# One hybrid decoder step: norm in five steps, old x loaded in two parts, the scan's filling work in token halves, state products over 128 rows

## The chip, the cores and the metric

The kernel runs on one core of one Trainium2 chip. The metric is the device time of one execution in microseconds, as the median over runs. A core has five engines that work through instruction lists of their own: TensorE (PE, matmuls; its weight loads are listed as PEld), VectorE (DVE), ScalarE (ACT), GpSimd (POOL) and SyncE (SP), which here only issues DMAs.

## The reference

One step of a decoder of two layers, for a prompt of 512 tokens and 8 sequences of 8 sample tokens, so T = 576 tokens in all, in fp32. Each layer is FFN, token mixer, FFN; the mixer of layer 0 is a Mamba-2 scan (SSD), that of layer 1 is windowed attention. Each of the six sublayers stands between two norms:

```python
hin = modulated_norm(x, norm_pre[i, s], mod[:, :, s])      # rms_norm, then scale and shift
f = swiglu(hin, w_in, w_out)                               # or ssd_mixer, or swa_mixer
x = x + FFN_RES * mod[:, :, s, 2] * rms_norm(f, norm_post[i, s])
```

In the scan, the prompt goes in 4 chunks of 128 tokens, and the 8 sample sequences start from states of their own. Per group of heads (4 groups) the state after a chunk is

```python
chunk_states = einsum('bclgn,bclgrp->bcgrpn', Bc, xc * decay_to_end[..., None])
hc = hc * a + s
```

and the outputs are y, the new states, the last conv inputs and the new key and value buffers.

## The kernel before

**Data and products.** Activations lie feature-major: 128 partitions by 8 feature blocks by tokens. The tokens are cut in two halves, HALF = ((0, 256), (256, 320)); the 64 sample tokens are the last ones of half 1. Each fp32 operand is split into a high and a low part, and a product is three matmuls (low weight by high activation, high by low, high by high); so a gemm of 8 blocks is 24 matmuls of one half's columns (line 501, output tile `g` in one of 4 PSUM buffers), and one of 6 blocks is 18. `load_w` brings a weight block from memory (tile `raw`, two buffers, issued on SP), ACT casts the high part (line 469) and DVE subtracts to get the low part (line 472); where the weights of several items are held at once, the tiles are called `wx` (otherwise `whi`, `wlo`).

**Who orders.** The Tile scheduler sets a fixed order for each engine at build time, by its own costs and by the order in which the code asks for things; at run time each engine goes through its list in that order and waits where an operand or a buffer is not there yet.

**A sublayer.** An FFN is four groups of feature tiles. The first goes through `run_in`: the weights of 8 items are held, all 8 are run over half 0, then all over half 1, and each gemm is followed by its `use`: for a gate, a Silu on ACT (line 724); for an up projection, a product on DVE (`sil`, 729), a cast on ACT (730) and a difference on DVE (`mid`, 731). The other groups go through `seven` (block products with fewer multiplications, line 673). The last group ends in `run_out` with r = 8: 8 blocks of w_out are held and run over half 0, then half 1; each result is added into `f` (566) and its sums of squares are begun (`stat`: lines 327 to 349, on ACT, POOL and DVE).

**The boundary.** Class `Boundary` leads from one sublayer to the next. `open` allocates tiles and loads the old x (1 MB for half 0, 1 MB for the first part of half 1, 256 KB for its samples, on SP, line 94); `stat`, `sums` form the norm's sums without waiting for the last product (gram matmuls of f and old x, line 343); `update(h)` adds f to x and writes the next sublayer's `hin` on DVE and ACT (lines 407 to 449). `update(0)` runs inside `run_out`, while PE works on half 1. `update(1)` runs inside the next `run_in`, ahead of its items in code: first the samples' part, then four pairs of feature blocks, each f times b1 (414), x plus f (415), two `pn` (436), two `hin` (438 on ACT, 439 on DVE):

```python
        if bd:
            bd.update(1)
            bd.close()
        for h in (0, 1):
```

PE meanwhile runs the items' half 0, which needs only half 0 of `hin`.

**The scan.** For each of 4 groups, a generator `mix` runs the scan's steps and yields nine times: after the B and C transposes, after each of 4 prompt chunks, after `old(0)`, `new(0)`, `old(1)` and `new(1)`. `old(q)` loads four sequences' states `h0` and multiplies C by them (`pos`, 994); `new(q)` makes their new states: for each sequence two matmuls over all sample tokens, the sequence picked by the mask in `bm`, into `psts` (1009 the high part, 1010 the low part over 64 rows), a scaling of h0 on POOL (1013) and a sum on DVE (1016). Between the yields the loop takes whole items from a list `fill`: projections of this and of the next group with their convolution (POOL copies at lines 846 to 867) and blocks of the output product. `gate_mul` and `gate_sum` (lines 1060 to 1075, sum of squares `gsq` by a matmul, 234) are called at two of these yields.

Of the kernel before, what the change touches and what calls it, by code (L numbers as in the profile page):

```python
# [10 lines left out]
F32 = mybir.dt.float32  # L11
# [30 lines left out]
PSP = 512  # L42
NX = 1
NG = 2
GK = 6
GJ = 2
GA = 0
GB = 1
GC = 1
# [9 lines left out]
def body(ctx: ExitStack, tc: tile.TileContext, A, O):  # L59
# [30 lines left out]

    def x_copy(d, x, store):
        for t, (o, n) in zip(x, XO):
            a, b = d[:, o:o + n], t.rearrange("p k n -> p (k n)")
            nc.sync.dma_start(a if store else b, b if store else a)
# [201 lines left out]
    class Boundary:  # L296
# [7 lines left out]

        def open(self):
            l, s = self.l, self.s
            state["xp_cm"] = tc.tile_pool(name=f"xpool{l}{s}", bufs=1, side="right", reuse_waits="tile")
            state["xp"] = state["xp_cm"].__enter__()
            x_cur[:] = x_alloc()
            x_copy(x_dram if l or s else A["xT"], x_cur, False)  # L310
            self.cms = [tc.tile_pool(name=f"{n}{l}{s}", bufs=1, side="right", reuse_waits="tile") for n in ("upd", "stats")]
            self.pool, pool = (cm.__enter__() for cm in self.cms)
            self.spool = pool
            mod_gate(l, s, self.mv)
            self.ns = 1 if self.end else 2
# [80 lines left out]

        def update(self, h):
            f, b1 = self.f, self.b1
            if not self.end:
# [3 lines left out]
            if self.end:  # L403
                return self.finish(h)
            if h == 1:
                ts = self.pool.tile([128, 8, 64], F32, tag="ts", name="ts", bufs=1)
                V.tensor_tensor(out=ts, in0=f[1][:, :, 256:320], in1=b1[:, 256:320].unsqueeze(1).to_broadcast([128, 8, 64]),
                                op=ALU.mult)
                V.tensor_tensor(out=x_cur[2], in0=x_cur[2], in1=ts, op=ALU.add)
                if not self.end:  # L410
                    norm_sample(self.pool, self.nmv, b2, self.hin)
            for kk in range(0, 8, 2):
                fs, xs = f[h][:, kk:kk + 2, 0:256], x_cur[h][:, kk:kk + 2, :]
                V.tensor_tensor(out=fs, in0=fs, in1=b1[:, 0:256].unsqueeze(1).to_broadcast([128, 2, 256]), op=ALU.mult)
                V.tensor_tensor(out=xs, in0=xs, in1=fs, op=ALU.add)
                if not self.end:
                    norm_prompt(self.pool, self.nmv, b2, self.hin, h, (kk, kk + 1))

        def finish(self, h):
# [97 lines left out]
    def run_in(hin, items, first, ex, pend, between=None, pre=()):  # L517
# [5 lines left out]
              for i, (src, _) in enumerate(items[:first])]  # L523
        if bd:
            bd.update(1)
            bd.close()
        for h in (0, 1):
            if between and h:
                between()
            for i, (w, (_, use)) in enumerate(zip(ws, items)):  # L530
                if h == 0 and i < len(pre):
                    use(h, gemm_part(w, hin_acts(hin, h), HALF[h][1], range(4, 8), pre[i][1]))
                else:
                    use(h, gemm(w, hin_acts(hin, h), HALF[h][1]))
            if bd and h == 0:
                bd.place(1, base)
        for src, use in items[first:]:
# [15 lines left out]
    def run_out(loads, acts, f, first, bd=None, r=0, ex=None, bias=None):  # L553
# [22 lines left out]
        if r:  # L576
            ws = [load_w(src, n, ex if i >= WR else None) for i, (src, n, _) in enumerate(loads[nl:])]
            todo = [(w, w0, o) for w, (_, _, os_) in zip(ws, loads[nl:]) for o, w0 in os_]
            for a in todo:
# [128 lines left out]
    def ffn(l, s, hin, f, pend, bd):  # L708
        si = 0 if s == 0 else 1
        sub = lambda name: tc.tile_pool(name=f"{name}{l}{s}", bufs=1, reuse_waits="tile")  # L710
        with sub("mid") as mp:
# [52 lines left out]
            with sub("tail") as tp:  # L764
                bd.open()
                run_out(loads, halves(mids), f, False, bd, RF, borrow(tp, "wf", 2 * (RF - WR), mk * 128))


    def ssd(l, hin, f, pend, bd):
        with ExitStack() as cx:  # L770
# [122 lines left out]
            def mix(g, d, y, sa, se, dtt, cd):  # L893
# [111 lines left out]
                def new(q, xh, xl):  # L1005

                    for b in range(q * 4, q * 4 + 4):
                        pst = ps_s.tile([128, 512], F32, tag="s", name="psts")
                        PE.matmul(out=pst, lhsT=bm[:, b, :], rhs=xh, start=True, stop=False)
                        PE.matmul(out=pst, lhsT=bm[0:64, b, :], rhs=xl, start=False, stop=True)  # L1010
                        h0 = h0s.pop(b)
# [4 lines left out]
                        V.tensor_tensor(out=h0, in0=pst, in1=h0, op=ALU.add)  # L1016
                        nc.scalar.dma_start(O["ssm_s"][g, :, b], h0)

                for i in range(5):
                    bcs(i)  # L1020
                yield
                h = None
                for i in range(4):
                    h = chunk(i, h)
                    yield
                skip(slice(0, NP))
                xd, pyv = within(4)
                old(0)
                yield
                xh = R2.tile([128, 512], F32R, tag="xdd", name="xh", bufs=2)  # L1030
                xl = R2.tile([64, 512], F32R, tag="xl", name="xl", bufs=1)
                S.copy(xh, xd)
                V.tensor_tensor(out=xl, in0=xd[0:64], in1=xh[0:64].bitcast(F32), op=ALU.subtract)
                new(0, xh, xl)
                yield
# [4 lines left out]
                yield  # L1040
                new(1, xh, xl)
                yield

# [58 lines left out]
            R = tc.tile_pool(name="ssdr", bufs=1, reuse_waits="tile")  # L1102
            Rcm, R = R, R.__enter__()
            def run1(item):
                run_in(hin, [item()], 0, None, pend)

# [12 lines left out]
            for g in range(4):  # L1119
                last = g == 3  # L1120
                fill = []
                outs = [lambda ld=ld, yn=yn: run_out([ld], yn_acts(yn), f, g == 1) for ld in out_loads(g - 1)] if g else []
                zt, ynew = [], []

                def z_run(j):
# [6 lines left out]
                    run1(lambda: z_item(g, j, zt[j]))  # L1132

                zs = [lambda j=j: z_run(j) for j in range(4)]
                dn, nxt = proj_items(g + 1) if not last else (None, [])
                nxt = [lambda it=it: run1(it) for it in nxt]
                fill = zs + outs if last else nxt[:NX] + outs + zs + nxt[NX:]
# [3 lines left out]
                steps = mix(g, d, y, *dd)  # L1141
                done = 0
# [24 lines left out]
            with tc.tile_pool(name="ssdo", bufs=1, reuse_waits="tile") as ap[0]:  # L1167
                bd.open()
                run_out(out_loads(3), yn_acts(yn), f, False, bd, 4)
# [516 lines left out]
```

## Time and profile before

| | before |
|---|---|
| median of 3 runs | 2581.92 us (2581.41 to 2588.04) |
| profiled execution | 2593.07 us, its span 2591.0 us |
| PE busy | 2493.8 us, 96% of the span |
| DVE busy | 1804.0 us, 70% |
| ACT busy | 1152.3 us, 44% |
| POOL busy | 202.8 us, 8% |
| mean granted TensorE clock in the span | 0.977 |

Busy is the sum of an engine's working time over the span of the profiled execution. PE is busy nearly always, so time can be found where PE stands still, where it works at the lower of its two clock levels (1.2 instead of 2.4 GHz; a window's granted clock of 0.5 is all at the lower one, 1.00 all at the upper one), or in PE's own work. In rows of the timeline the first number is the start, the second how long, and a bracket at the end says how long the engine stood idle before and what released it.

### The profile page before, as it was taken

How to read it: one execution, taken by the hardware profiler on the slowest of the kernel's cores; microseconds unless marked ns; L12 is line 12 of the kernel's file. 1: busy time of each engine (PE TensorE's matmuls, PEld its weight loads, DVE VectorE, ACT ScalarE, POOL GpSimd, SP SyncE). 2: the span in 40 equal slices, each digit the busy share in tenths (PEclk: the TensorE clock that was granted, in tenths of full speed). 3: DMA queues.
4: the chain of work that ended last, by engine and by line, in shares of the span. 5: the costliest groups of instructions: out<-in, count | busy, mean ns of one | idle time of the engine just before them, and what ended most of it. 6: DMA issues, size and time to landing. Idle time of an engine off the chain costs nothing.

```text
span 2591.0 us, 45688 instructions
## 1 busy us (share of the span) xinstructions
PE 2493.8 (96%) x18247; PEld 2309.2 (89%) x18247; DVE 1804.0 (70%) x3415; ACT 1152.3 (44%) x2396; POOL 202.8 (8%) x338
## 2 busy tenths in 40 slices
PE   6999999989999999999999999999999998999997
PEld 5999998877989878899999999999899788999997
DVE  5576766887768686667767757675766756577685
ACT  4343434554645454334424534342454664343343
POOL 1000000123131312000000100000010001000001
PEclk8999999999999999899999999999999998999998
DMA  7344534244444342344333343443436123233222
GB/s 261 106 167 135 191 134 167 94 117 130 122 131 107 131 115 107 120 138 127 122 135 120 121 139 107 167 177 126 168 124 202 34 70 107 94 101 103 91 94 110
DMA packets 119499, 331.04 MB, mean 128 GB/s; under 512 B 17903, under 2 KB 39903, under 8 KB 108671
## 3 DMA queue, kind: packets, MB, share of 16 engines
q1 hardware_dynamic: 100535, 245.46, 29.3%
q10 hardware_dynamic: 18752, 82.68, 9.3%
q8 instruction: 143, 2.34, 0.4%
q14 instruction: 69, 0.57, 0.1%
HBM read 301.63 MB, written 29.67 MB: 128 GB/s over the span
## 4 chain that ended last, share of the span: by engine, by line
PE 80%; DVE 8%; DMA 4%; ACT 3%; issue 3%; POOL 1%; SPq 0%; DVEq 0%; ACTq 0%; POOLq 0%
PE g L501 40%; PE g L673 29%; PE adaps L164 2%; DMA w<-scr_a 1%; PE gram L343 1%; DVE wlo L472 1%; DVE acc L863 1%; DMA raw<-in_w_out 1%; PE po L1298 1%; DVE hin L439 1%; PE py L947 1%; PE ssq L234 1%; DVE pn L436 1%; PE rb L255 1%; DMA x<-x_dram 1%
## 5 line engine op out<-in xcount | busy, mean ns | idle before, releaser
L501 PE MATMUL g<-hin,whi 128*128 128x320 f32 (+1 forms) x2528 | 533.4, 304 | 1.8 <-DVE hin L439 1.8
L501 PE MATMUL g<-mid,whi 128*128 128x320 f32 (+1 forms) x2432 | 489.3, 296 | 0.0
L673 PE MATMUL g<-hin,whi 128*128 128x288 f32 x2176 | 436.2, 294 | 0.0
L501 PEld LDWEIGHTS g<-hin,whi 128*128 128x128 f32 x2528 | 418.6, 194 | 10.3 <-issue 6.6
L501 PE MATMUL g<-hin,wlo 128*128 128x320 f32 (+1 forms) x1264 | 388.1, 309 | 16.1 <-ACT sil L724 7.0
L501 PEld LDWEIGHTS g<-mid,whi 128*128 128x128 f32 x2432 | 390.7, 188 | 1.1
L501 PE MATMUL g<-mid,wlo 128*128 128x256 f32 (+1 forms) x1216 | 359.8, 297 | 2.4 <-ACT mid L685 2.2
L673 PEld LDWEIGHTS g<-hin,whi 128*128 128x128 f32 x2176 | 349.1, 188 | 0.0
L673 PE MATMUL g<-tcmb,whi 128*128 128x288 f32 x1632 | 327.2, 294 | 0.0
L673 PE MATMUL g<-hin,wlo 128*128 128x288 f32 x1088 | 324.2, 298 | 0.0
L469 ACT CAST whi<-raw 128x1024 fp32r<-128x1024 f32 (+2 forms) x209 | 188.0, 900 | 236.3 <-PE g L501 162.5
L472 DVE TENSOR_TENSOR wlo<-raw,whi 128x1024 fp32r<-128x1024 f32 (+3 forms) x209 | 216.4, 1038 | 85.7 <-ACT whi L469 84.7
L501 PEld LDWEIGHTS g<-hin,wlo 128*128 128x128 f32 x1264 | 244.3, 194 | 33.7 <-issue 11.0
L673 PEld LDWEIGHTS g<-tcmb,whi 128*128 128x128 f32 x1632 | 262.5, 189 | 0.0
L673 PE MATMUL g<-tcmb,wlo 128*128 128x288 f32 x816 | 245.5, 301 | 0.0
L501 PEld LDWEIGHTS g<-mid,wlo 128*128 128x128 f32 x1216 | 228.6, 188 | 7.1 <-ACT mid L685 4.6
L652 ACT CAST whi<-scmb 128x512 fp32r<-128x512 f32 (+1 forms) x204 | 154.3, 760 | 160.8 <-PE g L673 83.5
L673 PEld LDWEIGHTS g<-hin,wlo 128*128 128x128 f32 x1088 | 204.1, 188 | 23.9 <-issue 23.9
L566 DVE TENSOR_TENSOR f<-g,f 128x256 f32<-128x256 f32 (+1 forms) x240 | 108.6, 455 | 143.4 <-PE g L501 142.2
L648 DVE TENSOR_TENSOR wlo<-scmb,whi 128x512 fp32r<-128x512 f32 (+1 forms) x204 | 175.6, 863 | 36.1 <-ACT whi L652 35.2
L673 PEld LDWEIGHTS g<-tcmb,wlo 128*128 128x128 f32 x816 | 153.3, 188 | 25.1 <-DVE ur L648 19.7
L652 ACT CAST whi<-raw 128x512 fp32r<-128x512 f32 x136 | 84.7, 623 | 166.2 <-PE g L673 98.4
(299 smaller groups left out, 3898.9 us busy)
## 6 DMA issues: line engine op xcount, KB each, us to landing
adaw<-in_ada_w ACTq DMA_DIRECT2D x56, 1024.0 KB, 5.4
raw<-in_w_in SPq DMA_DIRECT2D x108, 512.0 KB, 3.5
rawu<-in_w_in SPq DMA_DIRECT2D x68, 512.0 KB, 4.5
raw<-in_w_out SPq DMA_DIRECT2D x64, 384.0 KB, 3.1
raw<-in_w_out SPq DMA_DIRECT2D x64, 320.0 KB, 3.0
raw<-in_w_ssm SPq DMA_DIRECT2D x40, 512.0 KB, 3.5
x_dram<-x SPq DMA_DIRECT2D x10, 1024.0 KB, 3.9
x<-x_dram SPq DMA_DIRECT2D x10, 1024.0 KB, 6.3
```

What stands on the lines that cost most here:

```text
L164: PE.matmul(out=pt[32 * j:32 * j + 32, :w], lhsT=cs[:, k, :], rhs=aw[:, j * w:j * w + w], start=(k == 0), stop=(k == 7))
L234: ins = PE.matmul(out=ps[:, c0 + i:c0 + i + 1], lhsT=acc[:, o:o + 128], rhs=ones[:, 0:1], start=True, stop=True)
L255: ins = PE.matmul(out=r[:, c:e], lhsT=mul(y[:, i:i + 1], [128, 128]), rhs=ident[:, 128 - (e - c):128], start=True, stop=True)
L343: ins = PE.matmul(out=out, lhsT=a, rhs=b, start=(o == i == 0), stop=(o == 7), skip_group_check=True)
L436: V.scalar_tensor_tensor(out=tm, in0=x_cur[h][:, k, :], scalar=mv["gs"][:, k, 0:1], in1=r[:, :256], op0=ALU.mult, op1=ALU.mult)
L469: S.copy(hi[:, :n], raw[:, :n])
L472: i = (V if early and c < PSP else eng or V).tensor_tensor(out=lo[:, c:e], in0=raw[:, c:e], in1=hi[:, c:e].bitcast(F32), op=ALU.subtract)
L501: mms.append(PE.matmul(out=p[:, :n], lhsT=wt[:, a:b], rhs=at, start=(k == j == 0), stop=(j == 2 and k == K - 1)))
L566: V.tensor_tensor(out=fs, in0=p, in1=fs, op=ALU.add)
L648: e.tensor_tensor(out=out, in0=a, in1=b, op=op)
L652: S.copy(w[0][:, c:c + n], src)
L673: mms.append(PE.matmul(out=p, lhsT=wt[:, o], rhs=x, start=(first and k == j == 0), stop=(k == 3 and j == 2), skip_group_check=True))
```

## The change

It has four parts.

1. `Boundary.update` becomes a generator `updates`, which stops after the samples' part and after each of the four pairs. `run_in` asks for one step after each item of half 0, and for the rest after the last one. `update(0)` is as before.
2. `open` can load the first megabyte of the old x alone. At the ends of the four FFNs and of the SSD the other two parts are issued by `rest()`, after all w_out blocks of `run_out`. At the end of the attention everything is loaded at once, as before.
3. In the scan, `fill` holds token halves of items (and single output blocks) instead of whole items, and `mix` yields weights that sum up to 36, once per sequence in `new`. The shares before and after the places of `gate_mul` and `gate_sum` are scaled likewise (NX 1 to 2, NG 2 to 4, GB 1 to 3).
4. The tile `xl` has 128 rows, of which the upper 64 are set to zero by a DVE memset (four in all), and the low part's matmul goes over 128 rows.

The attention's boundary, the seven-product groups and all tile shapes but that of `xl` stay. The diff, cut:

```diff
+        def rest(self):
+            if self.more:
+                x_copy(*self.more, False, (1, 2))
+            self.more = None
-        def open(self):
+        def open(self, rest=True):
...
-            x_copy(x_dram if l or s else A["xT"], x_cur, False)
+            self.more = (x_dram if l or s else A["xT"], x_cur)
+            x_copy(*self.more, False, (0,))
+            if rest:
+                self.rest()
...
         def update(self, h):
+            for _ in self.updates(h):
+                pass
+        def updates(self, h):
...
                     norm_sample(self.pool, self.nmv, b2, self.hin)
+                yield
             for kk in range(0, 8, 2):
...
                     norm_prompt(self.pool, self.nmv, b2, self.hin, h, (kk, kk + 1))
+                yield
...
-        if bd:
-            bd.update(1)
-            bd.close()
+        steps = bd.updates(1) if bd else iter(())
         for h in (0, 1):
...
                     use(h, gemm(w, hin_acts(hin, h), HALF[h][1]))
+                next(steps, None)
             if bd and h == 0:
+                for _ in steps:
+                    pass
+                bd.close()
...
             ws = [load_w(src, n, ex if i >= WR else None) for i, (src, n, _) in enumerate(loads[nl:])]
+            bd.rest()
...
-                bd.open()
+                bd.open(False)
...
-                        PE.matmul(out=pst, lhsT=bm[0:64, b, :], rhs=xl, start=False, stop=True)
+                        PE.matmul(out=pst, lhsT=bm[:, b, :], rhs=xl, start=False, stop=True)
...
+                        yield 1
...
-                xl = R2.tile([64, 512], F32R, tag="xl", name="xl", bufs=1)
+                xl = R2.tile([128, 512], F32R, tag="xl", name="xl", bufs=1)
+                V.memset(xl[64:128].bitcast(F32), 0.0)
...
+            def pieces(item):
+                got = {}
+                def half(h):
+                    if h == 0:
+                        src, got["use"] = item()
+                        got["w"] = load_w(src, 1024)
+                    got["use"](h, gemm(got["w"], hin_acts(hin, h), HALF[h][1]))
+                    if h:
+                        pend.step()
+                return [lambda h=h: half(h) for h in (0, 1)]
...
-                for k, _ in enumerate(steps):
-                    while done < nfill * (k + 1) / 9:
+                done = k = 0
+                for part in steps:
+                    k += part
+                    while done < nfill * k / 36:
                         fill.pop(0)()
                         done += 1
-                    if k == GK:
+                    if k == 28:
                         acc = gate_mul(0, y, zt)
-                    if k == GK + 1:
+                    if k == 32:
                         r0 = gate_sum(0, acc)
```

How the engines' lists change is shown at three places. Line numbers of the changed program are some 8 to 18 higher.

**The end of an FFN.** SP's list where the last FFN group of layer 1's first FFN ends: `raw<-in_w_out` are the 8 held blocks, `x_...` the three parts of the old x. Before, then after:

```order
L467 DMA raw<-in_w_out 128x768 x6
L94 DMA x_20690<-x_dram 128x2048
L94 DMA x_20691<-x_dram 128x2048
L94 DMA x_20692<-x_dram 128x512
L467 DMA raw<-in_w_out 128x768 x2
```

```order
L482 DMA raw<-in_w_out 128x768 x6
L93 DMA x_20694<-x_dram 128x2048
L482 DMA raw<-in_w_out 128x768 x2
L93 DMA x_20695<-x_dram 128x2048
L93 DMA x_20696<-x_dram 128x512
```

The last two w_out blocks now stand behind one part of the old x instead of three. DVE's list at the same place, where `wx` are the blocks' low parts, `f` the results of half 0's products and `st` their sums; before, then after:

```order
L472 TENSOR_TENSOR wx<-raw,wx 128x768 x2
L566 TENSOR_TENSOR f_16469<-g,f_16469 128x256 x2
L349 TENSOR_TENSOR st_20703<-st_20703,stt 128x768 x2
L566 TENSOR_TENSOR f_16469<-g,f_16469 128x256
L349 TENSOR_TENSOR st_20703<-st_20703,stt 128x768 x2
L566 TENSOR_TENSOR f_16469<-g,f_16469 128x256
L472 TENSOR_TENSOR wx<-raw,wx 128x768 x2
```

```order
L487 TENSOR_TENSOR wx<-raw,wx 128x768 x2
L583 TENSOR_TENSOR f_16473<-g,f_16473 128x256 x2
L357 TENSOR_TENSOR st_20705<-st_20705,stt 128x768 x2
L487 TENSOR_TENSOR wx<-raw,wx 128x768
L583 TENSOR_TENSOR f_16473<-g,f_16473 128x256
L487 TENSOR_TENSOR wx<-raw,wx 128x768
L357 TENSOR_TENSOR st_20705<-st_20705,stt 128x768
```

The seventh block's `wx` moved ahead of two `f` and two `st`, the eighth's ahead of one `f` and two `st`. ACT's casts of the two blocks move forward in the same way, by eight instructions.

**The start of the FFN after a boundary.** DVE's list at the start of layer 1's first FFN, where `f`, `x`, `pn` and `hin` are the norm's steps for half 1, and `sil` and `mid` the `use` of half 0's up projections. Before:

```order
L415 TENSOR_TENSOR x_15835<-x_15835,f_11654 128x512
L439 SCALAR_TENSOR_TENSOR hin<-pn,modraw,hin 128x256 x2
L436 SCALAR_TENSOR_TENSOR pn<-x_15835,gs,rb 128x256 x2
L731 TENSOR_TENSOR mid<-sil,mid 128x256
L439 SCALAR_TENSOR_TENSOR hin<-pn,modraw,hin 128x256 x2
L729 TENSOR_TENSOR sil<-g,sil 128x256 x3
L731 TENSOR_TENSOR mid<-sil,mid 128x256 x3
```

and after:

```order
L429 TENSOR_TENSOR x_15839<-x_15839,f_11658 128x512
L454 SCALAR_TENSOR_TENSOR hin<-pn,modraw,hin 128x256 x2
L451 SCALAR_TENSOR_TENSOR pn<-x_15839,gs,rb 128x256 x2
L747 TENSOR_TENSOR sil<-g,sil 128x256
L454 SCALAR_TENSOR_TENSOR hin<-pn,modraw,hin 128x256 x2
L749 TENSOR_TENSOR mid<-sil,mid 128x256
L747 TENSOR_TENSOR sil<-g,sil 128x256
L749 TENSOR_TENSOR mid<-sil,mid 128x256
```

Of the four up projections of half 0, one `sil` and one `mid` stood ahead of the norm's last `hin` pair before; now three `sil` and two `mid` do. On PE, half 1's first two gemms, 24 matmuls in one piece each before, are now taken in turns (13 matmuls of the first, 1 of the second, 5, 5, 1, 4, 5 and the rest).

**The state products.** PE's list around `new(0)` of the first group, where `psts` are the new states of the sequences and `g` gemms of filling work. Before, and then after at its first and at its second to fourth sequence:

```order
L501 MATMUL g<-hin,whi 128x320 x2
L1009 MATMUL psts<-xh,bm 128x512
L1010 MATMUL psts<-xl,bm 128x512
L1009 MATMUL psts<-xh,bm 128x512
L1010 MATMUL psts<-xl,bm 128x512
L1009 MATMUL psts<-xh,bm 128x512
L1010 MATMUL psts<-xl,bm 128x512
L1009 MATMUL psts<-xh,bm 128x512
L1010 MATMUL psts<-xl,bm 128x512
L501 MATMUL g<-hin,wlo 128x256
```

```order
L516 MATMUL g<-hin,wlo 128x256
L516 MATMUL g<-hin,whi 128x256 x2
L1027 MATMUL psts<-xh,bm 128x512
L1028 MATMUL psts<-xl,bm 128x512
L516 MATMUL g<-hin,wlo 128x320
```

```order
L516 MATMUL g<-hin,whi 128x320 x2
L1027 MATMUL psts<-xh,bm 128x512
L1028 MATMUL psts<-xl,bm 128x512
L1027 MATMUL psts<-xh,bm 128x512
L1028 MATMUL psts<-xl,bm 128x512
L1027 MATMUL psts<-xh,bm 128x512
L1028 MATMUL psts<-xl,bm 128x512
L516 MATMUL g<-hin,wlo 128x256
```

The four sequences' products stood together; now half a filling item lies between the first and the others. On POOL, in three of the groups, the first `gacc` product of the gate now stands between the scalings of h0 instead of behind them all, and some copies of the convolution stand behind a scaling that they were ahead of.

## Rows read from the trace of the kernel before

**Rows 1.** The page's head: the span, busy time of each engine.

```profile
span 2591.0 us, 45688 instructions
PE 2493.8 (96%) x18247; PEld 2309.2 (89%) x18247; DVE 1804.0 (70%) x3415; ACT 1152.3 (44%) x2396; POOL 202.8 (8%) x338
```

**Rows 2.** Waits of PE: line, releaser, us in total, times, longest.

```profile
PE g L501 <- DVE wx L472: 12.9, 4, 3.6
...
PE gsq L234 <- DVE gacc L1066: 7.5, 6, 2.8
PE g L501 <- ACT sil L724: 7.0, 2, 3.7
...
PE g L501 <- ACT xpt L849: 3.1, 2, 2.6
```

**Rows 3.** Timeline of PE at the ends of three of the four FFNs.

```profile
444.33 6.95 PE L501 MATMUL g<-mid,wx 128*128 128x256 f32 x36 [3.59 <-DVE wx L472]
...
1891.80 4.48 PE L501 MATMUL g<-mid,wx 128*128 128x256 f32 x36
1899.53 6.07 PE L501 MATMUL g<-mid,wx 128*128 128x256 f32 x36 [3.25 <-DVE wx L472]
...
2549.32 5.89 PE L501 MATMUL g<-mid,wx 128*128 128x256 f32 x36 [2.68 <-DVE wx L472]
```

**Rows 4.** Timelines of SP's queue, ACT and DVE at the third FFN's end.

```profile
1885.32 2.16 SPq L94 DMA_DIRECT2D x<-x_dram  x3
1889.00 1.71 SPq L467 DMA_DIRECT2D raw<-in_w_out  x2
...
1896.72 0.81 ACT L469 CAST wx<-raw 128x768 fp32r<-128x768 f32 x1
...
1892.41 2.57 DVE L349 TENSOR_TENSOR st<-st,stt 128x768 f32<-128x768 f32 x2
...
1898.53 0.95 DVE L472 TENSOR_TENSOR wx<-raw,wx 128x768 fp32r<-128x768 f32 x1
```

**Rows 5.** DMA issues, count, KB, us to landing: whole page, then 1884 to 1900.

```profile
raw<-in_w_out SPq DMA_DIRECT2D x64, 384.0 KB, 3.1
...
raw<-in_w_out SPq DMA_DIRECT2D x3, 384.0 KB, 5.6
```

**Rows 6.** Timeline of PE at the starts of three FFNs.

```profile
1079.41 0.64 PE L501 MATMUL g<-hin,wlo 128*128 128x320 f32 x1 [3.26 <-ACT sil L724]
...
1500.35 11.42 PE L501 MATMUL g<-hin,wx 128*128 128x256 f32 x96
1515.47 0.63 PE L501 MATMUL g<-hin,wlo 128*128 128x320 f32 x1 [3.70 <-ACT sil L724]
...
2188.31 5.49 PE L501 MATMUL g<-hin,wx 128*128 128x256 f32 x24 [4.07 <-DVE sil L729]
```

**Rows 7.** Timeline of DVE at the second of these starts.

```profile
1514.84 0.87 DVE L439 SCALAR_TENSOR_TENSOR hin<-pn,modraw,hin 128x256 fp32r<-128x256 f32 x2
1515.64 1.07 DVE L729 TENSOR_TENSOR sil<-g,sil 128x256 f32<-128x256 f32 x3
```

**Rows 8.** Windows: stretch, length, busy PE, PEld, DVE, ACT, POOL, granted clock, DMA share, GB/s.

```profile
500.00:550.00 50.00, 39.88 (x250) 36.22 (x249) 45.35 (x92) 23.53 (x53) 13.10 (x26) 0.95 0.42 119
...
550.00:1000.00 450.00, 435.77 (x3051) 375.68 (x3050) 340.20 (x663) 225.35 (x553) 110.17 (x176) 0.98 0.43 126
```

**Rows 9.** Timeline of PE and PEld: 512-column products in the scan.

```profile
611.94 0.50 PE L1010 MATMUL psts<-xl,bm 64*128 64x512 f32 x1
612.36 0.50 PE L1009 MATMUL psts<-xh,bm 128*128 128x512 f32 x1
...
612.36 0.19 PEld L1009 LDWEIGHTS psts<-xh,bm 128*128 128x128 f32 x1 [0.24 <-issue]
612.79 0.18 PEld L1010 LDWEIGHTS psts<-xl,bm 64*128 64x128 f32 x1 [0.25 <-issue]
...
579.39 1.13 PE L970 MATMUL pst<-xdd,bt 128*128 128x512 f32 x2 [1.56 <-DVE xdd L929]
```

**Rows 10.** Waits in the scan, 550 to 1000: us in total, times, longest.

```profile
POOL h L1013 <- PE pos L994: 91.3, 11, 23.5
```

More of the change, by code (lines that the diff above doesn't have):

```diff
@@ L42 @@
 PSP = 512
-NX = 1
-NG = 2
-GK = 6
+NX = 2
+NG = 4
 GJ = 2
 GA = 0
-GB = 1
+GB = 3
 GC = 1
@@ L89, in body, with x_copy @@
     XO = ((0, 2048), (2048, 2048), (4096, 512))
-    def x_copy(d, x, store):
-        for t, (o, n) in zip(x, XO):
+    def x_copy(d, x, store, parts=(0, 1, 2)):
+        for t, (o, n) in ((x[i], XO[i]) for i in parts):
             a, b = d[:, o:o + n], t.rearrange("p k n -> p (k n)")
@@ L403, in update @@
             if self.end:
-                return self.finish(h)
+                self.finish(h)
+                return
             if h == 1:
@@ L1017, in new @@
                         nc.scalar.dma_start(O["ssm_s"][g, :, b], h0)
+                        yield 1
                 for i in range(5):
                     bcs(i)
-                yield
+                yield 4
                 h = None
@@ L1024, in mix @@
                     h = chunk(i, h)
-                    yield
+                    yield 4
                 skip(slice(0, NP))
@@ L1028, in mix @@
                 old(0)
-                yield
+                yield 4
                 xh = R2.tile([128, 512], F32R, tag="xdd", name="xh", bufs=2)
-                xl = R2.tile([64, 512], F32R, tag="xl", name="xl", bufs=1)
+                xl = R2.tile([128, 512], F32R, tag="xl", name="xl", bufs=1)
+                V.memset(xl[64:128].bitcast(F32), 0.0)
                 S.copy(xh, xd)
-                V.tensor_tensor(out=xl, in0=xd[0:64], in1=xh[0:64].bitcast(F32), op=ALU.subtract)
-                new(0, xh, xl)
-                yield
+                V.tensor_tensor(out=xl[0:64], in0=xd[0:64], in1=xh[0:64].bitcast(F32), op=ALU.subtract)
+                yield from new(0, xh, xl)
                 old(1)
@@ L1039, in mix @@
                 skip(slice(NP, T))
-                yield
-                new(1, xh, xl)
-                yield
+                yield 4
+                yield from new(1, xh, xl)
             def z_item(g, j, zt):
@@ L1103, in ssd, with out_pieces, one @@
             Rcm, R = R, R.__enter__()
+            def pieces(item):
[8 more added lines that the diff above has]
+                return [lambda h=h: half(h) for h in (0, 1)]
+            def out_pieces(ld, yn, first):
+                src, n, os_ = ld
+                got = {}
+                def one(i):
+                    if i == 0:
+                        got["w"] = load_w(src, n)
+                    o, w0 = os_[i]
+                    for h in (0, 1):
+                        p = gemm(got["w"], yn_acts(yn)(h), HALF[h][1], w0)
+                        if first:
+                            S.copy(f[h][:, o, :], p)
+                        else:
+                            V.tensor_tensor(out=f[h][:, o, :], in0=p, in1=f[h][:, o, :], op=ALU.add)
+                return [lambda i=i: one(i) for i in range(len(os_))]
             def run1(item):
-                run_in(hin, [item()], 0, None, pend)
+                for piece in pieces(item):
+                    piece()
             d, items = proj_items(0)
@@ L1121, in ssd, with z_make @@
                 fill = []
-                outs = [lambda ld=ld, yn=yn: run_out([ld], yn_acts(yn), f, g == 1) for ld in out_loads(g - 1)] if g else []
+                outs = [p for ld in out_loads(g - 1) for p in out_pieces(ld, yn, g == 1)] if g else []
                 zt, ynew = [], []
-                def z_run(j):
+                def z_make(j):
                     if not last:
@@ L1131, in z_run @@
                                   R.tile([128, 608], F32, tag="C", name="z", bufs=2)[:, 0:T])
-                    run1(lambda: z_item(g, j, zt[j]))
-                zs = [lambda j=j: z_run(j) for j in range(4)]
+                    return z_item(g, j, zt[j])
+                zs = [p for j in range(4) for p in pieces(lambda j=j: z_make(j))]
                 dn, nxt = proj_items(g + 1) if not last else (None, [])
-                nxt = [lambda it=it: run1(it) for it in nxt]
+                nxt = [p for it in nxt for p in pieces(it)]
                 fill = zs + outs if last else nxt[:NX] + outs + zs + nxt[NX:]
@@ L1141, in ssd @@
                 steps = mix(g, d, y, *dd)
-                done = 0
-                for k, _ in enumerate(steps):
-                    while done < nfill * (k + 1) / 9:
+                done = k = 0
+                for part in steps:
+                    k += part
+                    while done < nfill * k / 36:
                         fill.pop(0)()
                         done += 1
-                    if k == GK:
+                    if k == 28:
                         acc = gate_mul(0, y, zt)
-                    if k == GK + 1:
+                    if k == 32:
                         r0 = gate_sum(0, acc)
@@ L1167, in ssd @@
             with tc.tile_pool(name="ssdo", bufs=1, reuse_waits="tile") as ap[0]:
-                bd.open()
+                bd.open(False)
                 run_out(out_loads(3), yn_acts(yn), f, False, bd, 4)
```

## The prediction

> **What bounds the kernel now.** I read the page's head first: PE works 2493.8 of 2591.0 us [rows 1]. So some 97 us of standing still, the time at PE's lower clock, and PE's own work are all there is to win. PE's waits come second. The reader is to see that the largest, 12.9 us in only four waits, is for weights `wx` at the FFNs' ends, and that the 7.0 us for an ACT `sil` are only two [rows 2]: few long stalls, each at a known place. Third come the timelines at those places, where a stall is followed by slow matmuls. At the third FFN's end, 36 matmuls take 4.48 us ahead of the stall of 3.25 us and 36 of the same shape take 6.07 us behind it [rows 3]. So a stall here costs its length and then one to three us at the lower level. Last come windows over the scan, where no single wait is large.
>
> **Part 2, the ends of the FFNs.** What it can remove: the four stalls, 12.9 us [rows 2], and the slow matmuls behind them, 6.95 − 4.48, 6.07 − 4.48 and 5.89 − 4.48 us in the three shown [rows 3], on average 1.8, so some 7.3 us for four. Sum 20.2 us.
>
> Why PE waits: the seventh block is needed when the 36 matmuls of blocks five and six are through, at 1891.80 + 4.48 = 1896.28. Its load was issued at 1889.00, behind 2.25 MB of old x issued from 1885.32 on [rows 4], and took about 5.6 us instead of the usual 3.1 [rows 5]. ACT cast it at 1896.72, DVE subtracted at 1898.53 [rows 4], both in lists that place it behind sums. So two causes lie on top of each other, transfer and list. The change moves both: two parts of x now follow the weights, and the lists hold the casts earlier.
>
> With the usual 3.1 us the block lands at 1892.1 and the cast (0.81) ends at 1892.9. DVE's subtraction now follows the `st` pair, which ends at 1892.41 + 2.57 = 1894.98, so it ends at 1895.9, 0.4 us ahead of PE's need. The eighth comes one f (under 0.5) and one 0.95 us later, at 1897.3, and is needed 4.48 / 2 later, at 1898.5. The margin is thin, so the bounds are a stall of one `st` (1.3 us) or two and its slow matmuls in each end, at worst all four as now (gain 0), and 20. The parts of x that moved are asked for some 5 us later; half 1's gram products need them, after 36 more matmuls and the first of half 1, so the rest of half 0 hides them. If that cover were gone, the stall would come back as PE waiting for x. SP's next queue entries are the following sublayer's weights, wanted many us later. I take **20 us**.
>
> **Part 1, the starts of the FFNs.** The three stalls are 3.26, 3.70 and 4.07, together 11.0 us; the slow 24 matmuls behind the third take 5.49 where 24 of the row at full clock take 24 × 11.42 / 96 = 2.86, so 2.6 us each, 7.9 for three [rows 6]. Sum 18.9 us. Cause: DVE still had the norm to do until 1515.7, with the `use` of half 0's gemms behind it [rows 7], so all four PSUM buffers stayed full.
>
> Now two `sil` and a `mid` more stand ahead of the last `hin` pair, 3 × 0.36 us [rows 7], so `hin` is complete at 1516.8 instead of 1515.7. PE, no longer held, can start half 1 at 1500.35 + 11.42 = 1511.77. By then the first pair is there, and in its new order it takes the first two gemms' six ready blocks first, 36 matmuls of 11.42 / 96 × 320 / 256 = 0.149 us: up to 1517.1, just when the last pair arrives. I take **16 us** and leave 3 for small waits on single pairs. Bounds: 19, and 0 (the wait for `sil` becomes a wait for `hin`). The other users of `updates(1)` are the attention, whose `use` is on ACT and shows no such stall, so nothing, and the start of the SSD. There DVE works 45.35 of 50 us, PE stands still 10.1 us and loses 0.05 × 50 = 2.5 us to the clock [rows 8]. Interleaving puts convolution work between the norm's pairs, but the dt path and the first chunks come later with fewer gemms left to cover them. The most to win is 12.6 us; as much could be lost. I take **2 us**, bounds −8 and 8.
>
> **Part 4, the state products.** 32 sequences by two matmuls are 64 of 512 columns, 0.42 to 0.43 us apart where high and low alternate, and PE's weight loader stands idle 0.24 us ahead of each load [rows 9]. In a run of one shape, 256 columns take 11.42 / 96 = 0.119 us [rows 6], so 512 would take 0.24. From this row up to 64 × (0.43 − 0.24) = 12 us are to be had. The other bound is a same-shape row: two products of 512 columns in the prompt's states take 1.13 us [rows 9], no faster, gain 0. I take the first row as nearer, since its operands are split parts as here and the prompt's are unsplit, and of it **10 us**, since not every one of these 64 holds PE up. The four memsets are at most 4 × 0.87 us of DVE (two 128x256 steps each [rows 7]), in a stretch where DVE works 340 of 450 us [rows 8]; they cost nothing unless DVE is late, then up to 3.5.
>
> A rule speaks against it. The loads of 64 and of 128 rows take 0.18 and 0.19 us [rows 9]. The Trainium skill ("TensorE: Matmul & The Clock Gate", part 2, LDWEIGHTS, and part 3, the mechanism) says that a load's time goes by columns and not by rows, and that a load overlaps matmuls in flight only where the row groups differ. The equal loads agree with its first half; by the second, the switch to 128 rows would hide nothing and this part's gain would be 0. The gapless runs of full-height matmuls [rows 6] speak against that.
>
> **Part 3, the scan's filling.** Over 550 to 1000 PE stands still 14.2 us and loses 0.02 × 450 = 9 us to the clock [rows 8]: 23 us is the ceiling. Half of PE's stalls there are waits for `gacc` (7.5 us, six times, longest 2.8 [rows 2]); in three groups POOL's list now puts `gacc` between scalings. Finer filling also puts a gemm between dependent steps. Against it, at the first group's early chunks the filling comes in thinner. I take **5 us**, bounds −15 and 15.
>
> **Sum.** 20 + 16 + 2 + 10 + 5 = 53 us off the profiled execution: 2593.07 − 53 = 2540. That execution is 11.15 us above the median of 2581.92, so against the median the forecast is 2581.92 − 53 = 2529, set at **2530 us**.
>
> **Rivals.**
> - *The weights stay late.* The eighth-block margin of 1.2 us and the seventh's of 0.4 don't hold: a list entry ahead of `wx` waits for POOL's sums, and the four stalls and slow matmuls remain. For it: DVE's list, not the landing at 1894.6 (1889.00 + 5.6), came last. Against: the list moved too. Gain 33, 2549 us.
> - *Rows don't matter in the state products and the filling gives nothing.* 15 less, gain 38, 2544 us. The skill's rule above gives this, by its part 4 alone 2540.
> - *The norm only swaps its wait.* `hin` is late by more than its 1.1 us and PE stops for it at half 1's start, with the slow matmuls after. Gain 37, 2545 us.
> - *Slower: POOL's list in the scan.* The scalings of h0 wait for `pos`, 91.3 us in 11 waits, the longest 23.5 [rows 10], and everything behind them in POOL's list waits too. With `pos` matmuls now spread over half gemms, convolution copies and `gacc` stand behind them; the convolution then holds PSUM buffers and PE stops. It decides from 53 / 3 = 18 us in each of the three groups that have convolution to do; at one full wait of 23.5 us each, 70 us, less 53, the time is 2599 us. Against: in before these waits leave PE only 14.2 us idle in the whole stretch.
> - *The change does nothing at the FFNs' starts or ends because the scheduler restores the old lists.* The lists shown exclude this.
>
> **Chances.** Forecast 0.47; weights late 0.11; products and filling nothing 0.18; norm swaps 0.12; POOL 0.06; several of these at once, no change, 0.06. A measurement can tell about 0.3%, 7.7 us. So faster by more 0.88, within it 0.06, slower 0.06. The range takes in the upper bounds of single terms (parts 4 and 3 and the SSD's start together some 18 us more would be 2512) and the rivals' gains down to two of them together (53 − 20 − 15 = 18 would be 2564): 2510 to 2562.
>
> **What would show it.** Right: the four waits for `wx` at `run_out` gone from PE's waits, the 36 matmuls behind them in 4.5 us; no PE stop of over 1.5 us at the three FFN starts and a granted clock of 1.00 there; low and high state products about 0.24 us apart without loader idle; PE idle between 550 and 1000 (shifted) under 14 us; PE's busy sum lower. Wrong: waits for `hin` or x in place of these; state products still 0.4 us apart; POOL waits for `pos` followed by PE waits for `xpt`; the early part of the scan longer by more than 8 us.

## The result and the profile after

The changed kernel took 2542.09 us (median of 6 runs, 2534.73 to 2549.70) beside 2587.35 us of the kernel before: a ratio of 0.9827, 95% interval 0.9804 to 0.9851. That is 44.8 us less, 39 to 51 by the interval. In a second comparison, told below, the ratio was 0.984 (0.9824 to 0.9856, 2543.78 beside 2584.22 us), 41 us less. The forecast was 53 us less, 2530 us, with a range of 2510 to 2562. The direction and the range held. Of the five terms of its sum, one, part 2, was far off.

The page's head of the kernel after answers to [rows 1]:

```profile
span 2547.9 us, 45709 instructions
PE 2472.0 (97%) x18247; PEld 2298.1 (90%) x18247; DVE 1799.6 (71%) x3419; ACT 1153.6 (45%) x2396; POOL 210.7 (8%) x338
```

The span is 43.1 us shorter. PE's busy time fell by 21.8 us and its idle time from 97.2 to 75.9, so about half came out of stalls and half out of matmuls that run faster or follow each other more closely. PE's waits answer to [rows 2] (line, releaser, us in total, times, longest):

```profile
PE gram L351 <- ACT f L336: 7.3, 4, 2.2
PE py L965 <- DVE xdt L947: 4.9, 5, 1.9
PE pst L988 <- DVE xdd L947: 4.7, 1, 4.7
...
PE g L516 <- ACT hin L453: 4.2, 4, 1.6
PE pos L1012 <- DMA h<-in_h: 4.2, 5, 1.0
...
PE gsq L233 <- DVE gacc L1084: 1.4, 2, 0.8
```

The 12.9 us for `wx` and the 11 for `sil` are gone, and `gacc` fell from 7.5 to 1.4 us. The wait of gram for `f` has grown from 3.5 us (2.4 of them at the SSD's end, 0.3 to 0.5 at each of the first three FFN ends) to 7.3 (1.8 to 2.2 at each of these ends, where the first gram of half 1 waits). In the scan, the waits for `xdt`, `xdd` and h0's load have grown, from 1.2, 2.1 and 0.2 us to 4.9, 4.7 and 4.2.

**Where the 43 us came from.** The same PE instructions can be found in both traces, so the lead of the changed kernel can be read at each of them (start before minus start after). A stretch's gain is the growth of the lead.

| stretch | lead at its ends, us | gain |
|---|---|---|
| end of FFN 1 (first `wx` of half 0 to last `rb`) | −0.8 to 0.2 | 1.1 |
| SSD's start and scan | 0.2 to 15.8 | 15.6 |
| end of the SSD, update of half 0 | 15.8 to 18.1 | 2.3 |
| start of FFN 2 | 18.1 to 22.3 | 4.1 |
| end of FFN 2 | 22.2 to 22.0 | −0.1 |
| start of FFN 3 | 22.0 to 28.7 | 6.7 |
| end of FFN 3 | 30.7 to 30.8 | 0.1 |
| start of FFN 4 | 32.1 to 39.0 | 6.9 |
| end of FFN 4 | 39.0 to 43.1 | 4.1 |

The three FFN starts give 17.7 us against 16 forecast. The four FFN ends give 5.2 us against 20. This is the miss. It varies from one execution to the next: by the same measure the ends gain 5.6 to 10.2 us in the profiled executions of the other kernels below that have part 2 and not the late sum (among them the changed kernel again, 5.6). Some 3 us between these stretches, in FFN 3 and the attention, belong to no part of the change that I can name.

**What took the place of the stall at the FFN ends.** Timeline of PE at the end of FFN 2 after the change; it answers to [rows 3]:

```profile
1417.92 8.79 PE L516 MATMUL g<-mid,wx 128*128 128x256 f32 x72
...
1433.52 1.44 PE L351 MATMUL gram<-f,x 128*128 128x128 f32 x6 [1.82 <-ACT f L336]
```

The 72 matmuls that had a stall and a slow half now run through in 8.79 us: what the prediction said of `wx` holds. But 5 us after they end PE stops for the first gram. The windows behind that stop (columns as in [rows 8]):

```profile
1430.00:1435.00 5.00, 3.18 (x19) 2.57 (x17) 2.62 (x4) 3.02 (x6) 0.74 (x1) 0.88 0.09 19
1435.00:1440.00 5.00, 5.00 (x21) 5.00 (x22) 2.49 (x5) 2.58 (x7) 1.33 (x3) 0.50 0.39 134
1440.00:1445.00 5.00, 5.00 (x24) 4.66 (x24) 0.93 (x3) 0.05 (x1) 1.59 (x5) 0.60 0.15 60
```

The granted clock is 0.50 for one window and 0.60 in the next: PE works at the lower of its two levels, so here a stop of 1.82 us costs about 1.8 + 5 × 0.5 + 5 × 0.4 = 6 us. It isn't always so: in the run with part 4 undone, PE waits 2.03 us for gram at the end of FFN 3 (until 1884.37), and the granted clock is 1.00 in every window from 1885 to 1905. Why it stops is in DVE's timeline:

```profile
1427.87 0.96 DVE L357 TENSOR_TENSOR st<-st,stt 128x768 f32<-128x768 f32 x1 [0.64 <-POOL stt L343]
1428.74 0.42 DVE L583 TENSOR_TENSOR f<-g,f 128x256 f32<-128x256 f32 x1
1431.06 0.96 DVE L357 TENSOR_TENSOR st<-st,stt 128x768 f32<-128x768 f32 x1 [1.91 <-POOL stt L343]
1431.94 0.48 DVE L583 TENSOR_TENSOR f<-g,f 128x320 f32<-128x320 f32 x1
```

The last row is half 1's first product, which the gram needs after one more step on ACT. It stands in DVE's list behind the last `st` of half 0, which waits 1.91 us for POOL, which waits for ACT's `f`, which waits for the DVE addition at 1428.74, and that one stood behind the `st` before it, which again waited for POOL. Each block passes DVE, ACT, POOL and DVE again before the next block's addition may start. In the kernel before, the same chain stands in DVE's timeline at the end of FFN 3:

```profile
1905.41 0.96 DVE L349 TENSOR_TENSOR st<-st,stt 128x768 f32<-128x768 f32 x1 [1.91 <-POOL stt L335]
1906.29 0.42 DVE L566 TENSOR_TENSOR f<-g,f 128x256 f32<-128x256 f32 x1
1908.62 0.96 DVE L349 TENSOR_TENSOR st<-st,stt 128x768 f32<-128x768 f32 x1 [1.91 <-POOL stt L335]
1909.49 0.48 DVE L566 TENSOR_TENSOR f<-g,f 128x320 f32<-128x320 f32 x1
```

There PE, held up by its stop for `wx`, came to the gram so late that it waited only 0.50 us.

**The FFN starts.** Timeline of PE, then of DVE, at the start of FFN 3; they answer to [rows 6] and [rows 7]:

```profile
1478.31 11.43 PE L516 MATMUL g<-hin,wx 128*128 128x256 f32 x96
1489.57 0.31 PE L516 MATMUL g<-hin,wlo 128*128 128x320 f32 x1
```

```profile
1492.40 0.41 DVE L747 TENSOR_TENSOR sil<-g,sil 128x256 f32<-128x256 f32 x1
1492.73 0.87 DVE L454 SCALAR_TENSOR_TENSOR hin<-pn,modraw,hin 128x256 fp32r<-128x256 f32 x2
```

No stop, and no slow matmul behind. The last `hin` pair ends 1493.60 − 1478.31 = 15.3 us after PE's 96 matmuls began, in the kernel before 15.4: the 1.1 us that I added for the `use` between the pairs did not appear. FFN 2 kept one wait of 1.20 us for `hin`, the kind of wait that the lower bound named.

**The state products.** Timeline of PE and of the weight loader, as in [rows 9]:

```profile
608.65 0.39 PE L1027 MATMUL psts<-xh,bm 128*128 128x512 f32 x1
608.88 0.39 PE L1028 MATMUL psts<-xl,bm 128*128 128x512 f32 x1
...
608.89 0.19 PEld L1027 LDWEIGHTS psts<-xh,bm 128*128 128x128 f32 x1
609.12 0.19 PEld L1028 LDWEIGHTS psts<-xl,bm 128*128 128x128 f32 x1
```

They come 0.23 us apart, as extrapolated (0.24), and the loads shown have no idle time ahead of them. The windows of the scan, as in [rows 8]:

```profile
500.00:550.00 50.00, 44.53 (x310) 42.88 (x310) 49.45 (x101) 27.64 (x60) 24.31 (x30) 1.00 0.34 112
550.00:1000.00 450.00, 433.13 (x3113) 380.92 (x3112) 345.62 (x682) 233.68 (x570) 109.82 (x178) 0.99 0.43 128
```

### The profile page after: what moved, and what is told of

It is laid out like the page before. It is cut to its first block, busy times and chain, and to the rows that moved or that the text cites. A ratio compares the mean times of both kernels' runs of the same rounds, so it can differ in the third digit from the quotient of the medians.

```text
span 2547.9 us, 45709 instructions
## 1 busy us (share of the span) xinstructions
PE 2472.0 (97%) x18247; PEld 2298.1 (90%) x18247; DVE 1799.6 (71%) x3419; ACT 1153.6 (45%) x2396; POOL 210.7 (8%) x338
## 4 chain that ended last, share of the span: by engine, by line
PE 82%; DVE 7%; DMA 4%; ACT 3%; issue 2%; POOL 1%; SPq 0%; DVEq 0%; ACTq 0%; POOLq 0%
PE g L516 41%; PE g L691 29%; PE adaps L163 3%; DMA w<-scr_a 1%; PE gram L351 1%; DVE wlo L487 1%; PE ssq L233 1%; DVE acc L881 1%; PE py L965 1%; DVE st L357 1%; DMA out_ssm_s<-h 1%; PE rb L254 1%; PE po L1350 1%; DMA raw<-in_w_out 1%; PE g L504 1%
## 5 line engine op out<-in xcount | busy, mean ns | idle before, releaser
L516 PE MATMUL g<-hin,whi 128*128 128x320 f32 (+1 forms) x2528 | 521.8, 300 | 0.5 <-DVE hin L454 0.5
L516 PE MATMUL g<-hin,wlo 128*128 128x320 f32 (+1 forms) x1264 | 381.8, 306 | 10.1 <-ACT hin L453 4.2
L583 DVE TENSOR_TENSOR f<-g,f 128x256 f32<-128x256 f32 (+1 forms) x208 | 94.0, 455 | 129.4 <-PE g L516 128.4
```

What stands on the lines that cost most here:

```text
L516: mms.append(PE.matmul(out=p[:, :n], lhsT=wt[:, a:b], rhs=at, start=(k == j == 0), stop=(j == 2 and k == K - 1)))
L583: V.tensor_tensor(out=fs, in0=p, in1=fs, op=ALU.add)
```

## The experiments

First one part of the change was undone at a time. All ratios are to the kernel before on the same chip; a difference of two such ratios is uncertain by some 0.25 points, 6 us. The changed kernel was not timed again on the chip of the first four runs; for it stands the 0.984 of the second comparison. With the first one's 0.9827 each of these four differences is 0.13 points, 3 us, larger.

**Part 2 undone.**

```diff
-                bd.open(False)
+                bd.open()
```

> The changed kernel with part 2 undone: all three parts of the old x are loaded ahead of the w_out blocks again. Theory A (read from the two traces: at the first three FFN ends the stall for wx is replaced by a later one, PE waiting 1.8 to 2.2 us for the first gram of half 1 and then running some 5 us at the lower clock level, so that only the last FFN end gains): some 5 us slower than the changed kernel, about 2547 us; the stalls for wx return at all four ends and the waits of gram for f shrink from about 2 to about 0.4 us each at the first three. Rival B (part 2 is worth its 20 us and the waits of gram come from something else): some 20 us slower, about 2562 us, and the waits of gram stay at about 2 us.

Measured: 2550.32 us, ratio 0.9867 (0.9848 to 0.9887), so 0.27 points or 7 us slower than the changed kernel's 0.984 (10 us by the first ratio). PE's waits:

```profile
PE g L516 <- DVE wx L487: 13.3, 5, 3.6
...
PE gram L351 <- ACT f L336: 3.3, 4, 1.2
```

Theory A: the stall for `wx` is back and the wait of gram shrinks from 7.3 to 3.3 us. They trade places, though not to the full: the waits of gram at the first three ends are 0.9, 0.2 and 1.1 us here, where 0.4 was expected.

**Part 1 undone.**

```diff
-        steps = bd.updates(1) if bd else iter(())
+        if bd:
+            bd.update(1)
+            bd.close()
...
-                next(steps, None)
```

> The changed kernel with part 1 undone: half 1's norm is issued in one piece ahead of the items. Theory A: the three stalls at the FFN starts return with their slow matmuls, 17 to 18 us, and the SSD's start changes by 0 to 4; some 18 to 20 us slower than the changed kernel, about 2561 us. Rival B (the stalls went because the work around them moved, not by the steps): under 6 us slower, and no PE waits for sil over 2 us.

Measured: 2559.17 us, ratio 0.9899 (0.9878 to 0.992), 0.59 points or 15 us slower (19 by the first ratio). The stalls return where they were:

```profile
PE g L516 <- ACT sil L740: 6.9, 2, 3.8
PE g L516 <- DVE sil L745: 4.2, 1, 4.2
```

Theory A; 15 us is below its 18 to 20, 19 within. In the traces the three FFN starts gain 0.5 us without the steps and 17.7 with them. At the SSD's start the lead grew alike with and without the steps (by 5 and 6 us up to the first state product), so there part 1 is worth about 0 as long as part 3 is in. With both missing (part 2 alone, below) the lead falls by 1 us over that stretch; whether one of them stands in for the other was not tested.

**Part 4 undone.**

```diff
-                xl = R2.tile([128, 512], F32R, tag="xl", name="xl", bufs=1)
-                V.memset(xl[64:128].bitcast(F32), 0.0)
+                xl = R2.tile([64, 512], F32R, tag="xl", name="xl", bufs=1)
...
-                        PE.matmul(out=pst, lhsT=bm[:, b, :], rhs=xl, start=False, stop=True)
+                        PE.matmul(out=pst, lhsT=bm[0:64, b, :], rhs=xl, start=False, stop=True)
```

> The changed kernel with part 4 undone: the low part's state product over 64 rows, no memset. Theory A (each switch between 128 and 64 rows costs 0.2 us of PE, 64 of them, and PE is the bound in the scan): 12 to 13 us slower than the changed kernel, about 2555 us, and 0.42 to 0.43 us between the state products. Rival B (the time is covered because DVE or POOL sets the scan's pace): under 4 us slower.

Measured: 2551.64 us, ratio 0.9875 (0.9857 to 0.9893), 0.35 points or 9 us slower (12 by the first ratio). The loader's idle time is back, 0.24 to 0.25 us ahead of the loads shown:

```profile
608.29 0.19 PEld L1027 LDWEIGHTS psts<-xh,bm 128*128 128x128 f32 x1 [0.24 <-issue]
608.72 0.18 PEld L1028 LDWEIGHTS psts<-xl,bm 64*128 64x128 f32 x1 [0.25 <-issue]
```

Nearer to A than to B. The 64 × 0.2 = 12.8 us are a little too many: of the 44 distances between neighbouring state products in this run's trace, 29 are 0.41 to 0.43 us, but 15 are 0.32 or 0.33, all from the first high product behind a gemm to its low one. These lose 0.1 us each and not 0.2, so some 11 us are an estimate nearer to the trace, inside the 9 to 12 measured.

**Part 3 undone.**

```diff
-                for part in steps:
-                    k += part
-                    while done < nfill * k / 36:
+                for k, _ in enumerate(steps):
+                    while done < nfill * (k + 1) / 9:
```

(with whole items in `fill`, NX, NG, GK and GB as before).

> The changed kernel with part 3 undone: whole items as filling, nine equal shares, the old places of the gate. Theory A (the filling gave little: its waits for gacc were replaced by waits for xdd, xdt and h0): 0 to 4 us slower than the changed kernel, at most 2546 us, with the waits of gsq for gacc back at about 7 us. Rival B (finer filling is worth 6 us or more by itself): 6 to 12 us slower, about 2550 us.

Measured: 2545.34 us, ratio 0.9847 (0.9829 to 0.9865), 0.07 points or 2 us slower (5 by the first ratio), no difference that can be told. The wait for `gacc` is back as it was:

```profile
PE gsq L234 <- DVE gacc L1086: 7.5, 6, 2.8
```

Nearer to A, but B's 6 us are not excluded. One of A's reasons falls: the wait of `pst` for `xdd` is 4.2 us here too, and with part 1 undone it is 1.8 us in two waits, about as before the change (2.1), so it comes from part 1 at the SSD's start and not from the filling.

**The changed kernel again, part 2 alone, and a late running sum.** The third kernel tests the reading of DVE's list. It adds to the changed kernel that a block's sum is issued behind the next block's addition:

```diff
+                i = V.tensor_tensor(out=fs, in0=p, in1=fs, op=ALU.add)
...
-                V.tensor_tensor(out=self.acc[h][:, :ns], in0=self.acc[h][:, :ns], in1=st[:, :ns, :n], op=ALU.add)
+                self.late = lambda: V.tensor_tensor(out=acc[:, :ns], in0=acc[:, :ns], in1=st[:, :ns, :n], op=ALU.add)
+        def flush(self, other=None):
+            if self.late:
+                i = self.late()
+                if other is not None:
+                    behind(i, other)
+            self.late = None
```

where `stat` begins with `flush(i)`, `sums` with `flush()`, and `behind` fixes the order of two instructions in a list. The part-2-alone kernel is the kernel before with `rest()` and `open(False)`.

> The changed kernel itself, on the chip on which the next two are timed. Expected 40 to 47 us faster than before, and the three waits of gram at about 2 us each as in its first profile.

> The kernel before with part 2 alone (old x in two parts). Theory A (three of the four ends give back what the weights' earlier arrival wins, by a wait for the first gram of half 1 and the lower clock behind it): 2 to 6 us faster than before. Rival B (part 2 is worth its 20 us): 17 us faster or more.

> The changed kernel with one thing added: DVE's running sum of a block's squares is issued only behind the addition of the next block's product, so that the first product of half 1 no longer stands in DVE's list behind a sum that waits for POOL. Theory A (DVE's list makes PE wait at the three FFN ends): the waits of gram fall under 0.6 us each, the slow matmuls behind them go, and the time is 9 to 16 us less than the changed kernel's, about 2530 us. Rival B (ACT's or POOL's own pace, or the arrival of the old x, sets that wait): the waits of gram stay at 1.5 to 2 us and the time within 4 us of the changed kernel's.

Measured: the changed kernel 2543.78 us, 0.984 (0.9824 to 0.9856). Part 2 alone 2576.75 us, 0.997 (0.9959 to 0.9982), 7.8 us faster than before: between the theories, nearer to A, with this line among PE's waits:

```profile
PE gram L352 <- ACT f L337: 7.7, 4, 2.2
```

The late sum: 2525.80 us, 0.9769 (0.975 to 0.9788), 18 us less than the changed kernel on the same chip and 58 less than the kernel before. That is more than either theory said. Its profiled execution, the fastest of four, is 24 us shorter than the changed kernel's on that chip. At the three FFN ends PE no longer waits for gram at all. The end of FFN 2 on DVE:

```profile
1410.53 0.96 DVE L360 TENSOR_TENSOR st<-st,stt 128x768 f32<-128x768 f32 x1 [0.30 <-POOL stt L345]
1411.78 0.49 DVE L595 TENSOR_TENSOR f<-g,f 128x320 f32<-128x320 f32 x1 [0.30 <-PE g L527]
1412.19 0.95 DVE L360 TENSOR_TENSOR st<-st,stt 128x768 f32<-128x768 f32 x1
```

Half 1's first addition now waits for PE alone, and the sum comes behind it. The windows there:

```profile
1410.00:1415.00 5.00, 5.00 (x35) 4.55 (x34) 3.82 (x6) 3.87 (x8) 1.23 (x2) 1.00 0.02 10
1415.00:1420.00 5.00, 5.00 (x39) 4.75 (x40) 2.68 (x5) 2.56 (x7) 2.45 (x5) 1.00 0.50 188
```

PE is busy throughout, at full clock. From the first `wx` to the last `rb` the ends of FFN 1, 2 and 3 take 53.9, 53.8 and 54.5 us in the kernel before, 52.8, 53.9 and 54.5 in the changed one, and 48.4, 48.5 and 48.5 here. All four ends together gain 21 us on the kernel before, the size forecast for part 2. In PE's list the first gram even stands two matmuls earlier than in the changed kernel (behind 32 instead of 34 of half 1), so it is not a later place of the gram that helps. Another 3 us are at the start of FFN 2, which gained 6.9 us here and 4.1 in the changed kernel; what else differs between single executions can't be told from noise.

**Late sum without part 2, and on the kernel before.**

> The changed kernel with the running sum behind the next block's addition, but with part 2 undone (the old x whole, ahead of the last weights). Theory A (at an FFN's end two waits lie one behind the other, first wx, then gram; whoever takes away one alone meets the other): the stalls for wx return at about 2 to 3.5 us each, PE's gram hardly waits, and the time is 12 to 20 us more than with both, some 2540 to 2546 us, so that the late sum without part 2 gains only 4 to 10 us over the run with part 2 undone. Rival B (the late sum is worth its 18 us with or without part 2): about 7 us more than with both, some 2533 us.

> The kernel before with the late running sum alone. Theory A (two waits one behind the other): 0 to 8 us faster than before, the four stalls for wx still there at 2 us or more each. Rival B (worth its 18 us by itself): 15 us faster or more.

Measured: without part 2 2547.81 us, 0.9844 (0.9824 to 0.9864), so 0.23 points or 6 us better than part 2 undone alone, and 0.75 points or 19 us worse than with both. On the kernel before alone 2577.79 us, 0.9964 (0.9949 to 0.9979), 9.3 us faster. The waits for `wx`, of the first and of the second:

```profile
PE g L527 <- DVE wx L498: 12.2, 4, 3.4
```

```profile
PE g L512 <- DVE wx L483: 12.3, 4, 3.4
```

Theory A, although 9 lies just above its 0 to 8 us. On top of the other three parts, part 2 alone is worth 0.9867 − 0.984 = 0.27 points, 7 us, the late sum alone 0.9867 − 0.9844 = 0.23 points, 6 us, and both together 0.9867 − 0.9769 = 0.98 points, 25 us. On the kernel before, part 2 alone is worth 8 us and the late sum alone 9; both together were not run there. What the late sum wins on the kernel before lies mostly not at the FFN ends (1.9 us at most in one) but at the FFN starts, where its waits for `sil` fall from 11 to 6.8 us; that was not followed further.

## Why the prediction was right, and where not

- **Part 1: right.** 16 us forecast for the FFN starts; the trace shows 17.7 and undoing it costs 15 to 19. Stall and slow matmuls were priced from the right rows, and the new order of the first gemms covers the last `hin` pair as said.
- **Part 4: right.** 10 us forecast, 9 to 12 by undoing it, 0.23 us between the products. The row of 256 columns at one height was the right one to extrapolate from. The prompt's 512-column row, the lower bound, was misread: the code issues one product there, and the profile lists it as two matmuls, so the row prices one unsplit product and not two. The sentence of the Trainium skill (TensorE: Matmul & The Clock Gate, part 3, The mechanism) by which a load overlaps matmuls only where the row groups differ does not hold, taken by itself, in these rows: loads of 128 rows lie beside matmuls of 128 rows here. What agrees is the Trainium skill's TensorEngine Tiling (Array Packing), section Key Properties, by which a change of the tiling mode drains the engine: in the rows shown of the state products the loader is idle (0.24 to 0.25 us) at each change of height and has no idle time where the height stays.
- **Part 3: not decided.** 5 us forecast, 2 to 5 by undoing it, not to be told from 0 nor from the forecast. The waits for `gacc` went as said (7.5 to 1.4 us), but PE then waits for `xdt` and for h0's load instead (4.9 and 4.2 us in the profile, 2.3 and 3.1 in that of the second comparison). PE's idle time between 550 and 1000, which I expected under 14 us, is 450 − 433.13 = 16.9: that sign failed. The granted clock there is 0.99 instead of 0.98.
- **The SSD's start: right within its bounds**, 2 us forecast, about 0 by undoing part 1. The 2.3 us at the SSD's end were in no term. The wait of gram there fell from 2.4 to 1.2 us, in every variant but the late sum alone, with and without part 2; the cause stays open.
- **Part 2: wrong, 20 us forecast, 5 in the trace, 7 to 10 by undoing it.** The step that failed is the question of what is late next. I looked for it among the moved loads ("half 1's gram products need them, ... the rest of half 0 hides them"), and that held. What comes late is the gram's other operand, `f`: DVE's list holds half 1's first addition behind half 0's sums, and these run at the pace of a chain over DVE, ACT and POOL. The `st` pair of [rows 4], 2.57 us long, was a sign of it, and I used it to price `wx`; I did not follow the list on to half 1, where the trace of the kernel before shows the two waits of 1.91 us for POOL. Only the fourth end, which has no gram, gave its full share (4.1 us). With the late sum all four gave 21 us: the stalls for `wx` were priced rightly, and what was left out is the wait behind them.
- **Why the sum still fell in the range:** 53 less the 10 to 15 missing in part 2 is 38 to 43; measured were 41 and 45. That it came so near is partly luck: the SSD's end and the 3 us between the stretches, in no term of mine, add some 5 us, and the range was wide enough for two terms to fail.
- **The rivals.** That the weights stay late did not happen. POOL's waits for `pos` answer to [rows 10], and PE's waits for `xpt`, which they were to lengthen, came to 5.0 us, before 7.4:

```profile
POOL h L1031 <- PE pos L1012: 96.0, 18, 23.6
```

## What to carry to other kernels

When a stall is taken away, follow every in-order list beyond it up to the next point where the bounding engine needs something: two waits that lie one behind the other are worth little one by one (7 and 6 us here) and much together (25 us). An accumulation that waits for another engine should not stand in a list ahead of the instruction that empties the next product. And a stop of PE should be priced with the slow matmuls that may stand behind it, read from rows at both clock levels, and as a range: behind some stops here there were none.

## What was not expected of the hardware

- A stop of 1.82 us was followed by a granted clock of 0.50 in the next window and 0.60 in the one after, so the stop cost over three times its length. A stop's length alone does not tell: one of 2.03 us (part 4 undone, end of FFN 3) and one of 1.20 us (FFN 2's start) left the clock at 1.00, and one of 1.18 us at the SSD's end was followed by 0.50 (1005 to 1010).
- Multiplying 64 rows of zeros along is cheaper than leaving them out: 0.23 us for a 512-column product over 128 rows among its like, 0.42 to 0.43 over 64 rows among products over 128 (0.32 or 0.33 for the first pair behind a gemm).
